# A fourth chunk of x turned by VectorE blocks and carried inside SBUF by GpSimd's queue

## The chip, the cores and the metric

One Trainium2 chip, one core of it. The metric is device time in microseconds (us) for one launch; lower is better. Engines are named as the profile names them: PE (TensorE matmul), PEld (its weight load), DVE (VectorE), ACT (ScalarE), POOL (GpSimd), SP (SyncE, which here only issues DMAs; SPq is its queue).

## The reference

One layer of a hybrid encoder on x of 512 tokens by 2048 channels, all float32. What matters here is the head of it:

```python
def rms_norm(x, w):
    xf = x.astype(jnp.float32)
    y = xf * lax.rsqrt(jnp.mean(xf * xf, axis=-1, keepdims=True) + EPS)
    return (y * w.astype(jnp.float32)).astype(x.dtype)

def hybrid_layer(x, norm_w, w_in, ...):
    h = rms_norm(x, norm_w)                       # (1, 512, 2048)
    proj = jnp.einsum('bsd,de->bse', h, w_in)     # w_in is (2048, 4608)
    q, k, v, g_attn, xr, g_lru = jnp.split(proj, SPLITS, axis=-1)
    attn_out = attention_group(q, k, v, q_norm_w, k_norm_w)
    lru_out = lru_group(xr, conv_w, conv_b, ...)
    mixed = jnp.concatenate([rms_norm(attn_out, attn_norm_w) * jax.nn.silu(g_attn),
                             rms_norm(lru_out, lru_norm_w) * jax.nn.silu(g_lru)], axis=-1)
    return x + jnp.einsum('bse,ed->bsd', mixed, w_out)
```

## The kernel before

Every float32 product is made of three matmuls: both operands are split into a rounded high part and a low rest, and high by high, high by low and low by high are added up in PSUM (`mm3`, L152 to L155). The matmul contracts over the partitions, so x, which lies in memory with tokens on rows, has to be turned: 2048 channels become 16 tiles of 128 channels by 512 tokens. Two tiles are one **chunk**, so x has chunks 0 to 7, and so have the weights of a projection. Chunk c of x is loaded by `xload` (L234 to L241, 512 KB), chunk c of the weights by `wraw` (L206, 512 KB).

The first projection (`proj_feat` with C_XR, the loop at L1212) uses the chunks in order: chunks 0 and 1 by the lines L383 to L396, each later one as 24 matmuls of 512 columns (four column blocks e = 0 to 3 of six matmuls each, L401 to L406). It needs x as its loads arrive, so it begins at the start of the program; all later projections use the same turned x again. Its four sums stand in four PSUM banks named pj, which the second projection takes over when `evac_bc` (L464 to L473, the multiplication at L471) has read them.

There are two ways to turn a chunk:

- `xturn` (L249): PE transposes eight blocks of 128 by 128 into two PSUM banks (L253); ACT writes the high part of x times norm_w (L258), DVE the low part (L261). Chunks 0 to 4 go this way (`TURNED = 5`).
- by blocks (`xchunk`, L317 to L340), chunks 5 to 7: DVE turns blocks of 32 by 32 inside SBUF (`blocks`, L281, four instructions a chunk). What is left is to move blocks between groups of 32 partitions. `put_aside` (L289, tile xd) writes the chunk to HBM, and `bring_back` (L296, four DMAs) reads it back in the right order. Then ACT scales it by norm_w (L338, two instructions), ACT rounds the high parts and DVE subtracts the low ones (L339).

ACT and DVE split the weights: `wsplit` has a cast (L218, tile wh) and a subtraction (L219, tile wl) for each 128 rows. `behind` and `issue_after` only fix the order on an engine. The squares for the norm (`xsquare`) are made on DVE for chunks below TURNED (L272) and on ACT for the others (L268); `xstats` makes rstd from them (L373, L346, L347) and `rows` spreads it over the partitions with two matmuls (L367) into the tile rbc, which the multiplication at L471 needs.

The order around all this is written by hand. SP, PE, ACT and DVE stand in program order there, and the table `moves` (L1195) says what is emitted behind each step (c, e) of the first projection: "x5" advances the generator of chunk 5 to its next `yield`, "w5" issues the load of weight chunk 5, "s5" emits its split. SP issues its DMAs in that order; a DMA that has to wait holds up all behind it. In particular the four DMAs of `bring_back` wait until `put_aside` has landed.

Of the kernel before, what the change touches and what calls it, by code (L numbers as in the profile page):

```python
# [36 lines left out]
AHEAD = 600  # L37
# [12 lines left out]


B = 32
TURNED = 5
NQ = P // B


# [7 lines left out]
def hybrid_kernel(  # L64
# [20 lines left out]
    nc = tc.nc  # L85
# [57 lines left out]
    def mm():  # L143
        return ps.tile([P, SEQ], F32, tag="mm", name=nm("mm"))
# [4 lines left out]
    def f(ap):  # L149
        return ap.bitcast(F32)  # L150
# [7 lines left out]
    ident = const([P, P], "ident")  # L158
# [23 lines left out]
    nw = const([P, KT], "nw")  # L182
# [26 lines left out]
    turn_of, split_done = [0], {}  # L209
# [19 lines left out]

    xh, xl = [None] * KT, [None] * KT  # L230
    ssq = const([P, NT, KT // 2], "ssq")
    highs, x_parts, squared = {}, [], []

    def xload(c, nk=1):  # L234

# [7 lines left out]
    def behind(those):  # L243
        stack = ExitStack()
        for ins in those:
            stack.enter_context(tc.issue_after(ins))
        return stack

    def xturn(xc, kk, then=None):  # L249
        pt = mm()  # L250
        for t in range(NT):
            ks = slice(kk % 2 * P, (kk % 2 + 1) * P)
            nc.tensor.transpose(pt[:, t * P : (t + 1) * P], xc[:, t, ks], ident)  # L253
        if then:
            then()
        xh[kk], xl[kk] = x2(), x2()
        with behind(split_done[-1] if kk > 3 else ()):
            highs[kk // 2] = nc.scalar.activation(  # L258
                xh[kk], pt, AF.Identity, scale=nw[:, kk : kk + 1]
            ).ins  # L260
        nc.vector.scalar_tensor_tensor(  # L261
            xl[kk], pt, nw[:, kk : kk + 1], f(xh[kk]), op0=ALU.mult, op1=ALU.subtract
        )

    def xsquare(xc, c):
        for t in range(NT):
            if c >= TURNED:
                nc.scalar.activation(  # L268
                    xc[:, t, :], xc[:, t, :], AF.Square, accum_out=ssq[:, t, c : c + 1]
                )  # L270
                continue
            square = nc.vector.scalar_tensor_tensor(  # L272
                xc[:, t, :], xc[:, t, :], 1.0, xc[:, t, :], op0=ALU.mult, op1=ALU.mult,
                accum_out=ssq[:, t, c : c + 1],
            )
            if c == 1:
                squared.append(square.ins)

    def blocks(u, t, src):

        nc.vector.transpose(  # L281
            u[:, :, :, t, :].rearrange("p b k r -> p k b r"),
            src.rearrange("p (k b c) -> p k b c", k=2, c=B),
        )

    def put_aside(u, tag, bufs):

        aside_ = dram.tile([P, NQ, 2 * SEQ // NQ], F32, name=nm(tag), tag=tag, bufs=bufs)
        nc.sync.dma_start(aside_, u.rearrange("p b k t r -> p b (k t r)"))  # L289
        return aside_  # L290

    def bring_back(to, aside_):

        src = aside_.rearrange("(i c) b x -> b c i x", c=B)
        for b in range(NQ):
            nc.sync.dma_start(  # L296
                to[b * B : (b + 1) * B].rearrange("p i k t r -> p i (k t r)"), src[b]
            )

    def in_order(v):  # L300
        return v.rearrange("p (t i r) -> p i t r", t=NT, i=NQ)

    def xchunk(c):
# [16 lines left out]
        with tc.high_priority(AHEAD), tc.issue_after(squared[-1] if c == TURNED else split_done[3][1]):  # L320
            for t in range(NT):
                blocks(u, t, xc[:, t, :])
# [9 lines left out]
        with tc.high_priority(AHEAD), behind(split_done[-1]):  # L332
            for k in range(2):
                kk = 2 * c + k
                xh[kk], xl[kk] = x2(), x2()
                hi, lo = (in_order(v) for v in (xh[kk], xl[kk]))
                v = back[:, :, k]
                nc.scalar.activation(v, v, AF.Identity, scale=nw[:, kk : kk + 1])  # L338
                x_parts[:] = nc.scalar.copy(hi, v).ins, nc.vector.tensor_sub(lo, v, f(hi)).ins  # L339
        yield  # L340
# [11 lines left out]
    def rows(dst, col, dg):  # L352

        shape = [P, NT, P]
        part = [const([P, NT], nm("part")) for _ in range(2)]
        parts = [dg() for _ in part]
        nc.vector.tensor_copy(part[0].bitcast(F32R), col)
        nc.vector.tensor_sub(part[1], col, part[0])
        for c, d in zip(part, parts):
            nc.vector.tensor_mul(  # L360
                d, ident[:, None, :].broadcast_to(shape), c[:, :, None].broadcast_to(shape)
            )
        yield
        pb = mm()
        for k, d in enumerate(parts):
            d = d.rearrange("p t q -> p (t q)")
            nc.tensor.matmul(pb, ones_r, d, start=k == 0, stop=k == 1)  # L367
        nc.vector.tensor_copy(dst, pb)
        yield

    def xstats():
        s = const([P, NT], "xsum")
        nc.vector.reduce_sum(s, ssq, axis=AX.X)  # L373
        rsqrt_mean(rstd, s, DM, NT)
        yield from rows(rbc, rstd, lambda: k2(F32R, (P, NT, P)))


# [784 lines left out]
    s2 = ExitStack()  # L1162
# [28 lines left out]
    def split_x(c):  # L1191
# [1 line left out]
            given[c] = [wsplit(raws[c], k) for k in range(2)]  # L1193

    moves = {  # L1195
# [6 lines left out]
    }  # L1202

    def move(step):
# [7 lines left out]
    for step in proj_feat(C_XR, a1, first, given):  # L1212
        if step is None:
            with tc.high_priority():
                first.append(wsplit(raw, 1, nc.vector.tensor_copy))
                xturn(xc, 1)
            xsquare(xc, 0)
            move(None)
            given[1] = wload(w_in, 2 * P, C_XR)
            continue  # L1220
        c, e = step
        move(step)
        if (c, e) == (1, 2):
# [6 lines left out]
        if (c, e) in ((4, 3), (KT // 2 - 1, 0)):  # L1230
            with tc.high_priority(AHEAD), tc.issue_after(split_done[-1][1]):
                next(stats)

    s1.close()
# [214 lines left out]
```

## Time and profile before

| what | value |
|---|---|
| median of 3 runs | 627.18 us (627.06 to 629.06) |
| the profiled execution | 626.85 us |
| its span in the profile | 625.1 us, so 1.75 us lie outside of the span |
| granted TensorE clock | 0.999 |
| PE busy | 619.9 us |
| DVE, ACT, POOL busy | 494.5, 352.5, 101.7 us |

How to read the rows: a timeline row gives the start, the duration, the engine, the line of the kernel, the operation, the tile written and the tiles read, shapes, and how many instructions in a row were merged (x8); a bracket tells how long the engine had been idle before and what ended that. Buffer numbers are left out of tile names, so that every chunk of x is "b" when loaded, "xu" when in blocks, "xd" in HBM and "x" when split. Matmuls are pipelined: the distance between two starts says what one costs, not its duration. In rows of waits stand the total, the number of times and the longest.

### The profile page before, as it was taken

Reading aid. Unit: us, or ns where it says so; the run is one execution under the profiler, and the core shown is the slowest. Engines: PE = TensorE matmul, PEld = TensorE weight load, DVE = VectorE, ACT = ScalarE, POOL = GpSimd, SP = SyncE. Lnnn points to the kernel's source line nnn. Section 1 sums busy time; section 2 is a strip of 40 time slices with the busy share of each in tenths; the row PEclk is TensorE's granted clock in tenths of the full one; section 3 lists DMA queues with packets and bytes.
Section 4 is the critical chain, followed back from the end, with each engine's and each line's share of the span. In section 5 each row is a group of like instructions: output and inputs, shape, how many; then the busy total and the mean of one; then the engine's idle time right before and its main releaser. Section 6 shows DMA issues by size and latency. Waiting matters only on the chain.

```text
span 625.1 us, 8277 instructions
## 1 busy us (share of the span) xinstructions
PE 619.9 (99%) x2756; PEld 512.5 (82%) x2756; DVE 494.5 (79%) x796; ACT 352.5 (56%) x617; POOL 101.7 (16%) x134
## 2 busy tenths in 40 slices
PE   9999999999999999999999999999999999999997
PEld 7888888888888888888888888888888888888886
DVE  5967979986699875987887888549978866886886
ACT  3764899379935823555475447428445633443441
POOL 0000211112003622622122222100310101010010
PEclk9999999999999999999999999999999999999999
DMA  8987775859774599489668646923995676896262
GB/s 289 303 227 224 182 198 171 179 134 198 233 232 139 169 245 242 104 204 271 187 179 254 201 143 192 265 76 107 270 243 183 209 253 228 297 339 226 70 202 101
DMA packets 73595, 127.61 MB, mean 204 GB/s; under 512 B 6617, under 2 KB 29265, under 8 KB 73553
## 3 DMA queue, kind: packets, MB, share of 16 engines
q1 hardware_dynamic: 65664, 109.65, 56.8%
q0 software_dynamic: 7712, 17.31, 14.3%
q8 instruction: 21, 0.34, 0.2%
q14 instruction: 22, 0.17, 0.1%
q10 hardware_dynamic: 176, 0.14, 0.1%
HBM read 110.29 MB, written 37.75 MB: 237 GB/s over the span
## 4 chain that ended last, share of the span: by engine, by line
PE 99%; ACT 0%; DVE 0%; issue 0%; POOL 0%; POOLq 0%
PE pj L153 20%; PE pj L155 20%; PE pj L154 20%; PE mm L1029 14%; PE pj L1029 11%; PE mm L155 3%; PE mm L153 3%; PE mm L154 3%; PE pj L388 2%; PE mm L253 1%; PE mm L1156 0%; PE mm L829 0%; ACT x L258 0%; PE mm L367 0%; DVE cb L1058 0%
## 5 line engine op out<-in xcount | busy, mean ns | idle before, releaser
L153 PE MATMUL pj<-x,wh 128*128 128x512 f32 x368 | 143.5, 390 | 0.0
L155 PE MATMUL pj<-x,wl 128*128 128x512 f32 x368 | 143.2, 389 | 0.0
L154 PE MATMUL pj<-x,wh 128*128 128x512 f32 x368 | 143.2, 389 | 0.0
L218 ACT CAST wh<-wr 128x512 fp32r<-128x512 f32 x142 | 84.5, 617 | 79.3 <-PE pj L154 31.7
L219 DVE TENSOR_TENSOR wl<-wr,wh 128x512 fp32r<-128x512 f32 x144 | 99.5, 720 | 19.6 <-ACT wh L218 18.5
L881 ACT CAST wh<-wr 128x1024 fp32r<-128x1024 f32 (+1 forms) x72 | 60.7, 861 | 75.0 <-PE mm L1029 37.5
L882 DVE TENSOR_TENSOR wl<-wr,wh 128x1024 fp32r<-128x1024 f32 (+1 forms) x72 | 68.7, 984 | 30.3 <-ACT wh L881 30.0
L155 PEld LDWEIGHTS pj<-x,wl 128*128 128x128 f32 x368 | 69.1, 188 | 14.5
L154 PEld LDWEIGHTS pj<-x,wh 128*128 128x128 f32 x368 | 69.1, 188 | 14.3
L153 PEld LDWEIGHTS pj<-x,wh 128*128 128x128 f32 x368 | 69.1, 188 | 14.2
L153 PE MATMUL pj<-wh,x 128*128 128x512 f32 x192 | 74.7, 389 | 0.0
L155 PE MATMUL pj<-wh,x 128*128 128x512 f32 x192 | 74.7, 389 | 0.0
L154 PE MATMUL pj<-wl,x 128*128 128x512 f32 x192 | 74.7, 389 | 0.0
L905 POOL DMA_DIRECT2D t<-in_w_out_dram x40 | 33.6, 906 | 157.7 <-DMA t<-in_w_out_dram 99.9
L1029 PE MATMUL mm<-wh,ml 128*128 128x512 f32 x126 | 49.0, 389 | 0.0
L1029 PE MATMUL mm<-wh,mh 128*128 128x512 f32 x126 | 49.0, 389 | 0.0
L1029 PE MATMUL mm<-wl,mh 128*128 128x512 f32 x126 | 49.0, 389 | 0.0
L154 PEld LDWEIGHTS pj<-wl,x 128*128 128x128 f32 x192 | 36.0, 188 | 7.6
L155 PEld LDWEIGHTS pj<-wh,x 128*128 128x128 f32 x192 | 36.0, 188 | 7.5
L153 PEld LDWEIGHTS pj<-wh,x 128*128 128x128 f32 x192 | 36.0, 188 | 7.4
L706 POOL TENSOR_SCALAR p<-p,sm 128x512 f32<-128x512 f32 x32 | 24.3, 762 | 89.3 <-DVE sm L705 89.3
L1029 PE MATMUL pj<-wl,mh 128*128 128x512 f32 (+1 forms) x100 | 38.5, 385 | 0.0
(201 smaller groups left out, 1050.8 us busy)
## 6 DMA issues: line engine op xcount, KB each, us to landing
wr<-in_w_in_dram SPq DMA_DIRECT2D x71, 512.0 KB, 5.0
wr<-in_w_out_dram SPq DMA_DIRECT2D x24, 512.0 KB, 5.2
t<-in_w_out_dram POOLq DMA_DIRECT2D x40, 256.0 KB, 7.3
wr<-t SPq DMA_DIRECT2D x40, 256.0 KB, 5.6
pd<-u SPq DMA_DIRECT2D x16, 512.0 KB, 3.0
pt<-pd SPq DMA_DIRECT2D x64, 128.0 KB, 3.9
t<-in_w_out_dram SPq DMA_DIRECT2D x24, 256.0 KB, 5.3
t<-t SPq DMA_DIRECT2D x16, 256.0 KB, 5.4
```

Of the source, the lines that this page charges most:

```text
L153: nc.tensor.matmul(acc, lh, rh, start=start, stop=False)
L154: nc.tensor.matmul(acc, lh, rl, start=False, stop=False)
L155: nc.tensor.matmul(acc, ll, rh, start=False, stop=stop)
L218: copy(hi, raw[:, k, :]).ins,
L219: nc.vector.tensor_sub(lo, raw[:, k, :], f(hi)).ins,
L253: nc.tensor.transpose(pt[:, t * P : (t + 1) * P], xc[:, t, ks], ident)
L388: nc.tensor.matmul(acc[e], w[:, e * P : (e + 1) * P], x_[2 * c + k], start=c == k == j == 0, stop=False,)
L706: last_pool[0] = nc.gpsimd.tensor_scalar(p, p, sm, 0.0, op0=ALU.mult, op1=ALU.add).ins
L881: nc.scalar.copy(hi[:, to], b)
L882: nc.vector.tensor_sub(lo[:, to], b, f(hi[:, to]))
L905: nc.gpsimd.dma_start(dst, src, accum_op=ALU.add)
L1029: nc.tensor.matmul(dst[s][:, es], lh[:, ts_], rh[:, es], start=i == ends_[0] and j == 0, stop=i == ends_[1] and j == 2,)
```

## The change

Chunk 4 is turned by DVE's blocks as chunks 5 to 7 are (`TURNED = 4`), but `carry` moves its blocks from SBUF to SBUF: twelve DMAs of 32 KB on GpSimd's queue for the blocks that change their group of partitions, and four ACT copies for those that stay. Its squares are now made on ACT. The scaling by norm_w of chunks 4 to 7 is done by GpSimd (`tensor_scalar_mul`) instead of ACT. The first tile of x is transposed into two PSUM banks, and scaled and split in two halves of 256 tokens. The table `moves`, and with it the order of the loads, is written anew; the three chunks that go through HBM now go one after the other. In the first projection's last chunk the two matmuls of `rows` move from behind e = 0 to behind e = 1, where the transpose that makes `vec` stands; that one now stands ahead of them.

```diff
-TURNED = 5
+TURNED = 4
...
-    def xturn(xc, kk, then=None):
+    def xturn(xc, kk, then=None, n=1):
+        xh[kk], xl[kk] = x2(), x2()
+        ks = slice(kk % 2 * P, (kk % 2 + 1) * P)
+        parts_ = []
+        for h in range(n):
+            pt, w = mm(), SEQ // n
+            for t in range(NT // n):
+                nc.tensor.transpose(pt[:, t * P : (t + 1) * P], xc[:, h * NT // n + t, ks], ident)
+            cols = slice(h * w, (h + 1) * w)
+            with behind(split_done[-1] if kk > 3 else ()):
+                highs[kk // 2] = nc.scalar.activation(
+                    xh[kk][:, cols], pt[:, :w], AF.Identity, scale=nw[:, kk : kk + 1]
+                ).ins
+            parts_.append((pt[:, :w], cols))
...
+    def carry(to, u):
+
+        def at_(v, b):
+            return v[b * B : (b + 1) * B]
+
+        for d in range(1, NQ):
+            for b in range(NQ):
+                i = (b + d) % NQ
+                nc.gpsimd.dma_start(at_(to, b)[:, i], at_(u, i)[:, b])
+        with behind(split_done[2]):
+            for b in range(NQ):
+                nc.scalar.copy(at_(to, b)[:, b], at_(u, b)[:, b])
...
         with tc.high_priority(AHEAD):
-            there = put_aside(u, "xd", KT // 2 - TURNED)
-        with tc.issue_after(highs[TURNED - 1]):
-            xsquare(xc, c)
-        yield
-        with tc.high_priority(AHEAD):
-            bring_back(back, there)
+            if c == TURNED:
+                carry(back, u)
+            else:
+                there = put_aside(u, "xd", KT // 2 - TURNED - 1)
+                yield
+                bring_back(back, there)
...
-                nc.scalar.activation(v, v, AF.Identity, scale=nw[:, kk : kk + 1])
+                scaled[:] = (nc.gpsimd.tensor_scalar_mul(v, v, nw[:, kk : kk + 1]).ins,)
                 x_parts[:] = nc.scalar.copy(hi, v).ins, nc.vector.tensor_sub(lo, v, f(hi)).ins
...
-        xturn(xc, 0, split_first)
+        xturn(xc, 0, split_first, 2)
...
-        None: "x1", (0, 2): "x1",
+        None: "x1", (0, 2): "x1 x2 x4",
...
```

Where instructions stand now. First SP, from the load of weight chunk 4 (wr_383 before, wr_344 in the change) on. xd is a chunk on its way to HBM, "xu from xd" its way back; before, the chunks are 5 (xd_399), 6 (xd_431) and 7 (xd_437), and wr_405, wr_411 and wr_483 are the weights of chunks 5, 6 and 7:

```order
L206 DMA wr_383<-in_w_in_dram 128x2x512
L289 DMA xd_399<-xu_331 128x1024
L206 DMA wr_405<-in_w_in_dram 128x2x512
L296 DMA xu_332<-xd_399 32x4x256 x4
L206 DMA wr_411<-in_w_in_dram 128x2x512
L289 DMA xd_431<-xu_419 128x1024
L289 DMA xd_437<-xu_425 128x1024
L296 DMA xu_420<-xd_431 32x4x256 x4
L206 DMA wr_483<-in_w_in_dram 128x2x512
L296 DMA xu_426<-xd_437 32x4x256 x4
```

The same place in the change, where chunks 5, 6 and 7 are xd_378, xd_428 and xd_456, their weights wr_430, wr_454 and wr_492, b_61 is chunk 7 of x and wr_749 the first weights of the second projection:

```order
L206 DMA wr_344<-in_w_in_dram 128x2x512
L293 DMA xd_378<-xu_372 128x1024
L240 DMA b_61_386<-in_x_dram 128x4x256
L300 DMA xu_373<-xd_378 32x4x256 x4
L293 DMA xd_428<-xu_418 128x1024
L206 DMA wr_430<-in_w_in_dram 128x2x512
L300 DMA xu_419<-xd_428 32x4x256 x4
L206 DMA wr_454<-in_w_in_dram 128x2x512
L293 DMA xd_456<-xu_438 128x1024
L206 DMA wr_749<-in_w_in_dram 128x2x512
L300 DMA xu_439<-xd_456 32x4x256 x4
L206 DMA wr_492<-in_w_in_dram 128x2x512
```

Before, chunks 6 and 7 were put aside together, so that SP waited for two landings; in the change each chunk is put aside only when the one ahead of it has been asked back, and SP waits for three.

POOL, from its first DMA on, in the change (before, none of these rows stood ahead of the one that writes rstd):

```order
L312 DMA xu_256<-xu_255 32x256 x12
L367 TENSOR_SCALAR xu_256<-xu_256,nw 128x4x128 x2
L367 TENSOR_SCALAR xu_373<-xu_373,nw 128x4x128 x2
L367 TENSOR_SCALAR xu_419<-xu_419,nw 128x4x128 x2
L367 TENSOR_SCALAR xu_439<-xu_439,nw 128x4x128 x2
L379 TENSOR_SCALAR rstd<-xsum 128x4
```

Chunk 4's twelve DMAs and the eight scalings of chunks 4 to 7 came onto this queue.

Last DVE, where it reads the first projection's four banks (pj) into the tiles ev. Before:

```order
L471 TENSOR_TENSOR ev_694<-pj_159,rbc 128x512
L471 TENSOR_TENSOR ev_696<-pj_160,rbc 128x512
L471 TENSOR_TENSOR ev_698<-pj_161,rbc 128x512
L509 SCALAR_TENSOR_TENSOR k_122_706<-ev_694,vec,k_122_706 128x510
L471 TENSOR_TENSOR ev_700<-pj_162,rbc 128x512
```

In the change, from behind the copy of rbc on:

```order
L505 TENSOR_TENSOR ev_711<-pj_162,rbc 128x512
L534 TENSOR_TENSOR k_122_720<-k_113_699,k_121_719 128x512
L505 TENSOR_TENSOR ev_713<-pj_163,rbc 128x512
L543 SCALAR_TENSOR_TENSOR k_123_723<-ev_711,vec,k_123_723 128x510
L219 TENSOR_TENSOR wl_786<-wr_783,wh_785 128x512
L219 TENSOR_TENSOR wl_790<-wr_783,wh_789 128x512
L543 SCALAR_TENSOR_TENSOR k_123_723<-ev_711,vec,k_123_723 128x511
L505 TENSOR_TENSOR ev_715<-pj_164,rbc 128x512
L543 SCALAR_TENSOR_TENSOR k_123_723<-ev_711,vec,k_123_723 128x511
L505 TENSOR_TENSOR ev_717<-pj_165,rbc 128x512
```

The third read (ev_715) stood two instructions behind the first one; now it stands seven behind.

More of the change, by code (lines that the diff above doesn't have):

```diff
@@ L247, in behind @@
         return stack
-    def xturn(xc, kk, then=None):
[L250 to L253, printed above, removed]
+    def xturn(xc, kk, then=None, n=1):
[12 more added lines that the diff above has]
+            parts_.append((pt[:, :w], cols))
         if then:
             then()
[L256 to L259, printed above, removed]
+        for pt, cols in parts_:
+            lows[kk // 2] = nc.vector.scalar_tensor_tensor(
+                xl[kk][:, cols], pt, nw[:, kk : kk + 1], f(xh[kk][:, cols]),
+                op0=ALU.mult, op1=ALU.subtract,
             ).ins
-        nc.vector.scalar_tensor_tensor(
-            xl[kk], pt, nw[:, kk : kk + 1], f(xh[kk]), op0=ALU.mult, op1=ALU.subtract
-        )
     def xsquare(xc, c):
@@ L319, in xchunk @@
         )
[L320 removed]
+        raw_x[c] = xc
+        with tc.high_priority(AHEAD), behind(lows_of(c)):
             for t in range(NT):
[L322 removed]
+                blocked[c] = blocks(u, t, xc[:, t, :])
         yield
         with tc.high_priority(AHEAD):
[L325 to L327 removed]
+            if c == TURNED:
[4 more added lines that the diff above has]
+                bring_back(back, there)
+        if c == TURNED:
+            with tc.issue_after(highs[c - 1]):
+                xsquare(xc, c)
         yield
[L329 to L332 removed]
+        with tc.high_priority(AHEAD), behind(
+            (*split_done[-1], blocked[TURNED + 1]) if c == TURNED else split_done[-1]
+        ):
             for k in range(2):
@@ L337, in xchunk @@
                 v = back[:, :, k]
-                nc.scalar.activation(v, v, AF.Identity, scale=nw[:, kk : kk + 1])
+                scaled[:] = (nc.gpsimd.tensor_scalar_mul(v, v, nw[:, kk : kk + 1]).ins,)
                 x_parts[:] = nc.scalar.copy(hi, v).ins, nc.vector.tensor_sub(lo, v, f(hi)).ins
+        yield
+        for n in {5: (5, 6), 6: (7,)}.get(c, ()):
+            with behind(split_done[c][:1]):
+                xsquare(raw_x[n], n)
         yield
@@ L374, in xstats @@
         rsqrt_mean(rstd, s, DM, NT)
+        yield
         yield from rows(rbc, rstd, lambda: k2(F32R, (P, NT, P)))
@@ L1229, in hybrid_kernel @@
             columns(vec, vec_st)
-        if (c, e) in ((4, 3), (KT // 2 - 1, 0)):
-            with tc.high_priority(AHEAD), tc.issue_after(split_done[-1][1]):
+        if (c, e) in ((5, 3), (6, 3), (KT // 2 - 1, 1)):
+            with tc.high_priority(AHEAD), behind((split_done[-1][1], *scaled)):
                 next(stats)
```

14 lines of the change are left out of this document (8 added, 6 removed), and 10 rows, old and new, of the table moves.

## The prediction

> **What bounds the kernel now.** I read the page's busy times and chain first, then PE's waits, then the timeline of the first 56 us, where all changed instructions stand.
>
> ```profile
> PE 619.9 (99%) x2756; PEld 512.5 (82%) x2756; DVE 494.5 (79%) x796; ACT 352.5 (56%) x617; POOL 101.7 (16%) x134
> PE 99%; ACT 0%; DVE 0%; issue 0%; POOL 0%; POOLq 0%
> ...
> PE mm L1156 <- POOL ones L161: 1.1, 1, 1.1
> ```
>
> The second row is the chain that ended last, by engine; the third is the whole table of PE's waits. PE is busy from its first instruction to the end, and nothing but the first constant makes it wait. So a microsecond of PE work taken out is a microsecond won, and anything else matters only where it makes PE wait. After the 56 us discussed here the engines' orders are those of before but for a pair of DVE instructions, so I look for losses only there.
>
> **What is won.** The chunk that leaves PE:
>
> ```profile
> 22.39 0.39 PE L155 MATMUL pj<-x,wl 128*128 128x512 f32 x1
> 22.62 1.03 PE L253 MATMUL mm<-ident,b 128*128 128x128 f32 x8
> 23.41 0.48 PE L153 MATMUL pj<-x,wh 128*128 128x512 f32 x1
> ...
> 47.76 0.39 PE L155 MATMUL pj<-x,wl 128*128 128x512 f32 x1
> 47.99 0.39 PE L153 MATMUL pj<-x,wh 128*128 128x512 f32 x1
> ```
>
> Between two matmuls without transposes lie 0.23 us (47.76 to 47.99), with eight transposes 1.02 (22.39 to 23.41). Chunk 4's eight go: **−0.79 us**.
>
> The first tile's halves:
>
> ```profile
> 3.81 1.11 PE L253 MATMUL mm<-ident,b 128*128 128x128 f32 x4
> ...
> 4.71 0.85 PE L1156 MATMUL mm<-ones 128*128 128x256 bf16 x3
> 4.96 0.69 ACT L258 ACTIVATE x<-mm,nw 128x512 fp32r<-128x512 f32 x1 [2.25 <-PE mm L253]
> ...
> 5.70 1.23 PE L388 MATMUL pj<-x,wh 128*128 128x512 f32 x4
> ```
>
> ACT now waits for four transposes, then scales for 0.69 us, and PE starts 0.05 later. With halves it may begin two transposes earlier, and only half of the scaling stands behind the last one: at best half of 0.69, 0.35 us. An instruction on half the columns costs more than half, and the three warm-up matmuls hold PE until 5.56, so at worst 0.14 (5.70 to 5.56) or, if something else is late, nothing. I take **−0.2** (0 to −0.35). Both together: PE would be 0.99 ahead, and reach chunk 7 of the first projection at 47.99 − 0.99 = 47.0.
>
> **What may be late: the way through HBM.** In SP's timeline, L289 writes a chunk to HBM, L296 asks it back, L206 loads weights:
>
> ```profile
> 17.50 0.34 SPq L289 DMA_DIRECT2D xd<-xu  x1
> ...
> 24.77 1.76 SPq L296 DMA_DIRECT2D xu<-xd  x4
> 26.63 0.39 SPq L206 DMA_DIRECT2D wr<-in_w_in_dram  x1
> 27.12 0.88 SPq L289 DMA_DIRECT2D xd<-xu  x2
> 33.21 1.74 SPq L296 DMA_DIRECT2D xu<-xd  x4
> ...
> 35.55 1.83 SPq L296 DMA_DIRECT2D xu<-xd  x4
> ...
> SPq L296 <- DMA xd<-xu: 9.5, 2, 5.1
> pd<-u SPq DMA_DIRECT2D x16, 512.0 KB, 3.0
> ```
>
> The last two rows are SP's wait for the landing (twice), and the median landing of a later transfer of the same kind and size. Writing to asking back took 7.3 us behind a full queue (17.50 to 24.77) and 6.1 behind four reads and a load (27.12 to 33.21); alone it can be 3.0. What follows the asking:
>
> ```profile
> 29.28 1.34 ACT L338 ACTIVATE xu<-xu,nw 128x512 f32<-128x512 f32 x2 [0.20 <-DMA xu<-xd]
> ...
> 38.06 1.34 ACT L338 ACTIVATE xu<-xu,nw 128x512 f32<-128x512 f32 x2 [3.76 <-DMA xu<-xd]
> 39.30 1.13 ACT L339 CAST x<-xu 128x512 fp32r<-128x512 f32 x2
> 40.33 1.14 ACT L218 CAST wh<-wr 128x512 fp32r<-128x512 f32 x2
> 41.74 1.34 ACT L338 ACTIVATE xu<-xu,nw 128x512 f32<-128x512 f32 x2 [0.26 <-DMA vec_st<-in_lru_norm_w_dram]
> ```
>
> From asking to use are 4.5 us (24.77 to 29.28), 4.85 (33.21 to 38.06) and 6.2 (35.55 to 41.74, behind earlier reads and a load). From there to the weights' first cast, without which PE cannot begin the chunk, are 2.85 (38.06 to 40.33, and half of 1.14).
>
> Now the chain in the new order. Chunk 5's blocks stand on DVE behind the same splits as these seven of chunks 6 and 7 did, but for one block that stands earlier:
>
> ```profile
> 22.41 2.39 DVE L281 STREAM_TRANSPOSE xu<-b 128x256 f32<-128x256 f32 x7
> ```
>
> Ahead of ACT's casts there stand three of the new small copies, an estimated 0.3 us each; so the last three blocks (0.34 each) run from about 23.2 to 24.3. From there: write 3.0 (the queue is drained by then), 27.3; four reads issued, 1.85, and chunk 6 is put aside at 29.15. It lies behind those reads, so I take 4.2, between 3.0 and 6.1: asked back at 33.35. Reads and one load issued, 2.25: chunk 7 is put aside at 35.6. It lies behind four reads and a load, as the 6.1 did, but the load is later in the queue: 5.4 (3.0 to 7.3). Asked back at 41.0, landed after 4.7 (4.5 to 6.2) at 45.7, ready for PE 2.85 later at 48.55. PE is there at 47.0: **+1.55 us of waiting**. With all low ends the chunk is ready at 44.75 and nothing waits; with all high ends at about 54, 7 us late. Chunk 5, by the same steps ready at 34.9, and 6, ready at 40.9, are due at 36.1 and 41.55: hidden, with about a microsecond to spare.
>
> GpSimd scales instead of ACT:
>
> ```profile
> L905 POOL DMA_DIRECT2D t<-in_w_out_dram x40 | 33.6, 906 | 157.7 <-DMA t<-in_w_out_dram 99.9 <-issue 39.1 <-DMA t<-t 18.5
> L706 POOL TENSOR_SCALAR p<-p,sm 128x512 f32<-128x512 f32 x32 | 24.3, 762 | 89.3 <-DVE sm L705 89.3
> ...
> L1053 POOL DMA_DIRECT2D out_dram<-xt x6 | 3.4, 572 | 74.5 <-DVE xt L1104 57.4 <-DVE xt L1058 17.0
> ...
> t<-in_w_out_dram POOLq DMA_DIRECT2D x40, 256.0 KB, 7.3
> ...
> out_dram<-xt POOLq DMA_DIRECT2D x6, 256.0 KB, 4.0
> ```
>
> Two scalings of 0.76 us take the place of ACT's 1.34, and ACT's first cast runs beside the second: nothing, so the 2.85 stays. ACT's freed time has no price either, nor have the extra squares there: it was idle for 3.76 us before the second use above.
>
> **Chunk 4's carrying.** Its blocks follow the squares of chunk 1:
>
> ```profile
> 14.40 0.42 DVE L272 SCALAR_TENSOR_TENSOR b<-b 128x256 f32<-128x256 f32 x1
> ...
> 16.05 1.42 DVE L281 STREAM_TRANSPOSE xu<-b 128x256 f32<-128x256 f32 x4 [1.23 <-DMA b<-in_x_dram]
> ```
>
> DVE is free at 14.8 (the four blocks before waited 1.23 us for an x that is now one place later in the queue), so they are done at 16.2. A DMA issue on POOL costs 0.572 us for a plain write out of SBUF and 0.906 for an adding one in HBM; landing takes 4.0 and 7.3. None of before goes from SBUF to SBUF with 32 KB. I take the plain row, which it is nearest to: 16.2 + 12 × 0.572 + 4.0 = 27.1, and with 2.85 ready at 29.95; due at 47.99 − 0.99 − 3 × 24 × 0.227 = 30.7. Hidden by 0.7. By the other ends 16.2 + 10.9 + 7.3 + 2.85 = 37.2, 6.5 us late.
> [...] No row of before shows POOL's queue beside a full one.
>
> **The reading of the banks.** The second projection needs the four pj banks one after the other, 6 × 0.227 = 1.36 us apart.
>
> ```profile
> 49.35 0.62 PE L367 MATMUL mm<-k,ones_r 128*128 128x512 f32 x2
> 50.01 0.69 DVE L368 COPY rbc<-mm 128x512 f32<-128x512 f32 x1 [3.89 <-PE mm L367]
> ...
> 52.59 1.87 DVE L471 TENSOR_TENSOR ev<-pj,rbc 128x512 f32<-128x512 f32 x3
> 54.39 0.74 DVE L509 SCALAR_TENSOR_TENSOR k<-ev,vec,k 128x510 f32<-128x510 f32 x1
> 55.05 0.68 DVE L471 TENSOR_TENSOR ev<-pj,rbc 128x512 f32<-128x512 f32 x1
> ```
>
> The copy of rbc begins 0.66 after the pair of matmuls. Call X the start of the change's transpose ahead of that pair, which costs about 0.1: the copy starts at X + 0.76. DVE's steps are 0.6 to 0.66 apart by these rows, so the third read, eight steps on, ends at about X + 6.4. PE has the pair (0.46) and 12 matmuls, and is at the second projection's third block at X + 0.56 + 24 × 0.227 = X + 6.0: **+0.4 us** (0 to 1). Before, the fourth read ended at 55.7, and PE came to that bank at about 58. Whether X itself is late doesn't matter to this.
>
> **Sum** against the profiled execution of 626.85 us (the span of 625.1 and 1.75 around it): −0.79 − 0.2 + 1.55 + 0.4 = +0.96, 627.8. The median of the runs shown lies 0.33 above that execution, so I forecast **628.2**. About 0.3% (1.9 us) is what a measurement can tell from no change.
>
> **Rivals.**
> 1. *The trips fit.* If each write lands as the 3.0 row says, chunk 7 is ready in time; what is left is −0.99 and +0.4: 626.3, or 626.6 on the median. For it speaks that a write from SBUF is quick alone; against, that both trips in the trace took over 6.
> 2. *GpSimd's queue is the late one.* Twelve issues follow one another on one engine, and the chunk is due 14.5 us after its blocks. It turns the sum to slower by more than 0.3% once the blocks land after about 30.2, that is 14.0 us behind the last DVE block, or 0.83 us an issue with a landing of 4.0. With 0.906 and 7.3 it is 6.5 late: 626.85 − 0.99 + 0.4 + 6.5 = 632.8, on the median 633.1. For it: 40 of POOL's DMAs cost 0.906. Against: those add in HBM.
> 3. *The trips are as long as those measured* (6.1 and 7.3 for the second and third): ready at 24.3 + 3 + 1.85 + 6.1 + 2.25 + 7.3 + 4.7 + 2.85 = 52.35, 5.35 late; 631.6, on the median 631.9.
> [...]
>
> **How the numbers follow.** Forecast 0.50; rival 1 0.22; rival 2 0.12; rival 3 0.13; rival 4 0.03. The range 626.0 to 630.6 goes from rival 1 with the halves worth 0.35 and a cheap bank reading to the parts of rivals 2 and 3 that are less than half as bad as written; their worse parts and rival 4 stay out. Slower by over 0.3%: rival 4, and most of 2 and 3, 0.25; faster 0.01, since no more than 1.14 us is to be won; the same 0.74.
>
> **What would show it.** No transposes inside the first projection's chunk 2 (22.62 above); its first matmul near 5.5; SP asking chunks 5, 6, 7 back near 27, 33 and 41; PE waiting for ACT ahead of chunk 7 and for DVE at the second projection's third bank. [...] The forecast is wrong if chunk 5 or 6 is already late, or if PE waits anywhere after 60 us.

## The result, and the profile after

The changed kernel takes **634.49 us** (median of 5 runs, 633.9 to 635.12), the kernel before 627.18 beside it: a ratio of 1.0109 (95% interval 1.0094 to 1.0124), 1.1% slower. The forecast was 628.2, with a range up to 630.6. In the profiled execution the span grew from 625.1 to 632.0 us, 6.9 us.

The page of the changed kernel, busy times and chain:

```profile
PE 622.2 (98%) x2748; PEld 511.7 (81%) x2748; DVE 495.6 (78%) x793; ACT 352.1 (56%) x624; POOL 121.4 (19%) x154
...
PE 90%; DMA 2%; DVE 1%; POOL 1%; issue 1%; ACT 0%; SPq 0%; POOLq 0%; ACTq 0%; DVEq 0%
```

PE has eight matmuls less and is busy 2.3 us longer, and the chain has left PE for a tenth of the span. The table of PE's waits had one entry before; now (total, times, longest):

```profile
PE pj L153 <- ACT wh L218: 3.4, 2, 2.5
PE mm L1190 <- POOL ones L161: 1.1, 1, 1.1
PE pj L422 <- ACT x L259: 0.4, 1, 0.4
PE pj L1063 <- DVE ev L505: 0.4, 1, 0.4
PE pj L153 <- DVE ev L505: 0.4, 1, 0.4
PE mm L256 <- DMA b<-in_x_dram: 0.2, 1, 0.2
```

The two waits for ACT's casts of weights stand ahead of chunk 5 (1.0 us) and of chunk 7. The waits for ev are the second projection's third bank and a bank at 477 us; the rest lies at the start. PE's timeline around the second, and the clock there (busy times by engine, then PEclk, the DMA share and GB/s):

```profile
48.80 0.39 PE L155 MATMUL pj<-x,wl 128*128 128x512 f32 x1
51.71 0.50 PE L153 MATMUL pj<-x,wh 128*128 128x512 f32 x1 [2.52 <-ACT wh L218]
52.05 0.53 PE L154 MATMUL pj<-x,wh 128*128 128x512 f32 x1
...
53.10 0.63 PE L153 MATMUL pj<-x,wh 128*128 128x512 f32 x1
53.53 0.63 PE L154 MATMUL pj<-x,wh 128*128 128x512 f32 x1
...
55.62 0.39 PE L153 MATMUL pj<-x,wh 128*128 128x512 f32 x1
55.86 0.39 PE L154 MATMUL pj<-x,wh 128*128 128x512 f32 x1
```

```profile
53.00:54.00 1.00, 1.00 (x4) 0.71 (x4) 1.00 (x5) 0.21 (x1) 0.00 (x0) 0.50 1.10 323
...
56.00:58.00 2.00, 2.00 (x11) 1.61 (x10) 1.35 (x5) 0.10 (x1) 0.00 (x0) 1.00 0.97 291
```

Between 48.80 and 51.71 PE loses 2.7 us, and then the matmuls come 0.43 us apart instead of 0.23: the granted clock is 0.50 until about 55.5. So the wait is followed by a second loss: the next nine distances take 3.91 us in all (51.71 to 55.62), where 9 × 0.227 = 2.04 is usual. How much of these 1.87 us is the clock's, the first experiment shows.

What made chunk 7 late, on SP (put aside, a load of the second projection, asked back), GpSimd (scaling) and ACT (casts):

```profile
36.12 0.41 SPq L293 DMA_DIRECT2D xd<-xu  x1
38.93 0.38 SPq L206 DMA_DIRECT2D wr<-in_w_in_dram  x1
42.83 1.74 SPq L300 DMA_DIRECT2D xu<-xd  x4
```

```profile
16.52 4.11 POOL L312 DMA_DIRECT2D xu<-xu  x8 [14.82 <-DVE xu L285]
22.68 1.96 POOL L312 DMA_DIRECT2D xu<-xu  x4 [2.05 <-DMA xu<-xu]
26.24 3.12 POOL L367 TENSOR_SCALAR xu<-xu,nw 128x512 f32<-128x512 f32 x2 [1.59 <-DMA xu<-xu]
...
47.38 3.10 POOL L367 TENSOR_SCALAR xu<-xu,nw 128x512 f32<-128x512 f32 x2 [5.50 <-DMA xu<-xd]
```

```profile
48.98 0.62 ACT L368 CAST x<-xu 128x512 fp32r<-128x512 f32 x1 [3.79 <-DMA vec_st<-in_lru_bx_dram]
50.52 0.62 ACT L368 CAST x<-xu 128x512 fp32r<-128x512 f32 x1 [0.92 <-POOL xu L367]
51.04 2.17 ACT L218 CAST wh<-wr 128x512 fp32r<-128x512 f32 x4
```

Two scalings take 3.10 us, and ACT's second cast waits for the second one. The 6.9 us of the span, against the terms of the forecast:

| term | forecast | measured |
|---|---|---|
| PE begins chunk 7 (47.99 before) | 48.55 | 51.71 |
| of that: put aside at | 35.6 | 36.12 |
| put aside to asked back | 5.4 | 6.71 (36.12 to 42.83) |
| asked back to first use | 4.7 | 4.55 (42.83 to 47.38) |
| first use to PE | 2.85 | 4.33 (47.38 to 51.71) |
| nine slow distances after the wait | none | +1.87 |
| second projection's third bank | +0.4 | +0.53 |
| wait for a bank at 477 us | none | +0.53 |

Chunk 7 begins 3.72 later than before (51.71 against 47.99): 3.72 + 1.87 + 0.53 + 0.53 = 6.65. The other 0.25 is spread over small gaps. Against the forecast, chunk 7 is 3.16 late: 0.52 by the putting aside, 1.31 by the trip, 1.48 from first use to PE, and −0.15 by the way back.

### The profile page after: what moved, and what is told of

Same layout as the page of the kernel before. It is cut to its first block, busy times and chain, and to the rows that moved or that the text cites. A ratio compares the mean times of both kernels' runs of the same rounds, so it can differ in the third digit from the quotient of the medians.

```text
span 632.0 us, 8307 instructions
## 1 busy us (share of the span) xinstructions
PE 622.2 (98%) x2748; PEld 511.7 (81%) x2748; DVE 495.6 (78%) x793; ACT 352.1 (56%) x624; POOL 121.4 (19%) x154
## 4 chain that ended last, share of the span: by engine, by line
PE 90%; DMA 2%; DVE 1%; POOL 1%; issue 1%; ACT 0%; SPq 0%; POOLq 0%; ACTq 0%; DVEq 0%
PE pj L153 19%; PE pj L155 19%; PE pj L154 19%; PE mm L1063 13%; PE pj L1063 11%; PE mm L155 3%; PE mm L154 3%; PE mm L153 3%; DMA xd<-xu 1%; POOL xu L367 1%; DMA xu<-xd 0%; DVE wl L219 0%; DVE b L278 0%; DVE ev L505 0%; SPq L300 0%
## 5 line engine op out<-in xcount | busy, mean ns | idle before, releaser
L1063 PE MATMUL pj<-wh,mh 128*128 128x512 f32 (+1 forms) x100 | 38.6, 386 | 0.4 <-DVE ev L505 0.4
```

Source lines behind the costliest of these rows:

```text
L1063: nc.tensor.matmul(dst[s][:, es], lh[:, ts_], rh[:, es], start=i == ends_[0] and j == 0, stop=i == ends_[1] and j == 2,)
```

## The experiments

Each quoted block says what was expected of a run. Times are medians, with the lowest and the highest in brackets.

### Scaling back on ACT, and a PE that isn't left idle

```diff
-                scaled[:] = (nc.gpsimd.tensor_scalar_mul(v, v, nw[:, kk : kk + 1]).ins,)
+                nc.scalar.activation(v, v, AF.Identity, scale=nw[:, kk : kk + 1])
```

> The changed kernel with the scaling of chunks 4 to 7 back on ACT, all else kept. Theory A (GpSimd's scaling is dear, 1.56 us each where I had 0.76, and stands on the path of chunks 5 and 7): chunk 7's first cast of weights comes 2.85 us after the chunk's last landing instead of 4.3, so PE begins chunk 7 about 1.5 us earlier (50.2 instead of 51.7); the wait ahead of chunk 5 (1.0 us) goes, but that time only moves into the wait ahead of chunk 7, which stays at 2.5 us or more, with the low clock behind it. About 633.0 us. Rival B (both waits cost their own): 631.5 us. Rival C (the scaling is beside other work, as I forecast): 634.5 us.

And, between chunks 6 and 7:

```diff
+        if (c, e) == (6, 3):
+            warm = mm()
+            busy(20)
```

> The changed kernel with 20 matmuls of 128x256 bf16 on constants, whose result nobody reads, on PE between chunks 6 and 7 of the first projection, where it waits 2.5 us in the changed kernel. Theory A (the low granted clock of 0.5 from 52 to 55.6 us comes from PE's idle time just before, and doubles the time of the ten matmuls that follow, 0.43 us apart instead of 0.23): these run 0.23 apart, the clock stays at 1.0, and the kernel is 2.0 us faster, 632.5 us. Rival B (the ten matmuls are slow because transfers, casts and splits of weights run beside them): nothing changes, 634.5 us, or slower if the 20 matmuls take longer than the wait (0.11 to 0.23 us each, 2.2 to 4.6 us).

Measured: 633.2 us (631.56 to 635.83) with ACT's scaling, 633.08 (632.04 to 633.54) with the 20 matmuls. PE in the latter:

```profile
50.90 2.36 PE L1190 MATMUL mm<-ones 128*128 128x256 bf16 x20
53.01 0.48 PE L153 MATMUL pj<-x,wh 128*128 128x512 f32 x1
53.32 0.40 PE L154 MATMUL pj<-x,wh 128*128 128x512 f32 x1
53.55 0.39 PE L155 MATMUL pj<-x,wl 128*128 128x512 f32 x1
```

Chunk 7's matmuls come 0.23 apart, with the same casts and transfers beside them, so these did not make them slow; rival B is out. That the idle time did is likely, but this run alone doesn't show it: in this execution chunks 5 and 6 were later, PE came to chunk 7 at 50.90 instead of 49.03, and the wait would have been about 1.3 us only (ACT's first cast of the weights began at 51.57, and PE starts 0.67 behind it in the changed kernel). The 20 matmuls held PE until 53.01, some 0.8 longer, and so only 1.4 us of the 2.0 appear in the time.

With ACT's scaling the wait ahead of chunk 5 went (0.16 left), but chunk 7 began at 51.53, not at 50.2: asked back at 42.88, it was used only from 48.60 on, 5.7 us later instead of 4.55. A 0.6 us wait ahead of chunk 6 was new, since ACT's scaling there stood behind eight squares, and the second projection's bank made PE wait 1.35 us instead of 0.53. The clock, after a wait as long as before (48.62 to 51.53):

```profile
53.00:54.00 1.00, 1.00 (x6) 0.80 (x5) 1.00 (x4) 0.04 (x1) 0.00 (x0) 1.00 0.00 0
```

It stayed at 1.00, where the changed kernel had 0.50. The nine distances behind the wait took 2.65 us here (51.53 to 54.18), 0.61 over the usual at full clock; by this comparison some 1.3 of the 1.87 us are the clock's. The low clock follows such a wait in one execution (0.50) and not in another (1.00), so the 1.3 us won on the median can't be put down to the scaling alone. Theory A had the right sum by a partly wrong way.

### Which form of the scaling

```diff
-                scaled[:] = (nc.gpsimd.tensor_scalar_mul(v, v, nw[:, kk : kk + 1]).ins,)
+                scaled[:] = (nc.gpsimd.tensor_scalar(
+                    v, v, nw[:, kk : kk + 1], 0.0, op0=ALU.mult, op1=ALU.add
+                ).ins,)
...
-        last_pool[0] = nc.gpsimd.tensor_scalar(p, p, sm, 0.0, op0=ALU.mult, op1=ALU.add).ins
+        last_pool[0] = nc.gpsimd.tensor_scalar_mul(p, p, sm).ins
```

> The changed kernel with GpSimd's two kinds of scaling exchanged: chunks 4 to 7 by a multiply and an add of zero (the form of the scaling of p in the attention, 0.7 us), p by a multiply alone (the form used for the chunks, 1.56 us). Theory A (the form of the instruction makes the difference): the chunks' scaling takes 0.7 to 0.8 us, that of p 1.5, and the attention is later for it. Rival B (the way through memory makes it, four pieces of 128 elements instead of 512 in a row): the chunks' scaling stays at 1.55 us, p's at 0.7. Rival C (transfers or DVE beside it make it): neither stays as it was.

GpSimd's groups (busy time, mean ns of one), in the changed kernel and with the forms exchanged:

```profile
L740 POOL TENSOR_SCALAR p<-p,sm 128x512 f32<-128x512 f32 x32 | 24.2, 760 | 89.6 <-DVE sm L739 89.6
L367 POOL TENSOR_SCALAR xu<-xu,nw 128x512 f32<-128x512 f32 x8 | 13.2, 1658 | 12.6 <-DMA xu<-xd 11.1 <-DMA xu<-xu 1.6
```

```profile
L742 POOL TENSOR_SCALAR p<-p,sm 128x512 f32<-128x512 f32 x32 | 52.8, 1654 | 83.7 <-DVE sm L741 81.4 <-PE pj L154 2.3
...
L367 POOL TENSOR_SCALAR xu<-xu,nw 128x512 f32<-128x512 f32 x8 | 6.3, 801 | 17.3 <-DMA xu<-xd 15.7 <-DMA xu<-xu 1.6
```

Theory A is shown, on both tiles: the multiply alone takes twice as long as the multiply with an added zero (1658 against 801 ns for the chunks, 1654 against 760 for p, on average). The attention pays for it (651.5 us, one run). My row for the forecast, 762 ns, was of the other form.

With only the chunks' form put right, and the multiplications that read the banks given precedence:

```diff
-        with tc.high_priority():
+        with tc.high_priority(2 * AHEAD):
             for n, a in enumerate(acc):
```

> The changed kernel with one word of its edit put right: chunks 4 to 7 scaled on GpSimd by a multiply and an add of zero (0.8 us) instead of a multiply alone (1.56 us), and the bank reads given precedence on DVE. The way through HBM stays as the change has it. Theory A (the scaling is 1.5 us of chunk 5's and of chunk 7's path, the third trip the rest): the wait ahead of chunk 5 shrinks from 1.0 to 0.5 us or less, PE begins chunk 7 at 50.2 to 50.7 instead of 51.7 after a wait that is still over 2 us; with the bank's 0.5 won, 632.5 us where that wait brings the low clock and 631 where it doesn't. Rival B (the transfers alone set when chunk 7 comes): no more than the bank's 0.5 is won, 634 us.

Measured: 633.34 us (632.91 to 633.48). The wait ahead of chunk 5 is gone and the second projection's bank waits no more. But chunk 7, asked back at 43.35, was used from 49.40 on, and PE waited 3.2 us for it; the mean granted clock of this execution was 0.997, as in the changed kernel. The time lies between theory A's 632.5 and rival B's 634; PE begins chunk 7 at 51.98, as late as before, and in this rival B is right: the transfers set when chunk 7 comes.

### Fewer trips in a row

Chunks 6 and 7 put aside together, as in the kernel before, with x's chunk 7 loaded earlier and later loads of weights held in place; then the same with ACT's scaling:

```diff
-        (2, 0): "x6 w4 x4", (2, 1): "x5 x5", (2, 2): "x7", (2, 3): "s3 x4",
-        (3, 0): "x6 x5 x6 w5", (3, 1): "x7 x6", (3, 2): "w6 x7", (3, 3): "s4 x5",
-        (4, 0): "x7 w7", (4, 3): "s5 x5 x6",
+        (2, 0): "x6 x7 w4 x4", (2, 1): "x5 x5", (2, 3): "s3 x4",
+        (3, 0): "x6 x7 x5 x6 w5 x7", (3, 1): "x6", (3, 2): "w6 x7", (3, 3): "s4 x5",
+        (4, 0): "w7", (4, 3): "s5 x5 x6",
```

> The changed kernel with chunks 6 and 7 put aside one right after the other (x's chunk 7 loaded earlier, its blocks behind those of chunk 6; two loads of weights held behind the load for chunk 6 and the last read of chunk 7), so that the way through HBM is made two times after one another instead of three. GpSimd still scales. Theory A (the third trip in a row, asked back at 42.8 us, is what makes chunk 7 late): SP asks chunk 7 back at about 37.5, PE does not wait ahead of it, the clock stays at 1.0, and only the wait ahead of chunk 5 (1.0 to 1.5 us, by GpSimd's scaling), the second projection's bank and 0.5 late in the kernel are left: 629 us (628 to 630.5). Rival B (the bytes ahead in the queue set it, not the number of trips): chunk 7 lands as late as before, 634 us.

> As the kernel with chunks 6 and 7 put aside together, and the scaling back on ACT. Theory A (the two named costs, trip and scaling, are all that makes PE wait in the first projection): no wait above 0.3 us ahead of chunks 4 to 7, 0.8 us of transposes won, and the second projection's bank (0.5 us) left: 627.0 us, within 0.3% of the kernel before. Rival B (carrying chunk 4 or the other order of casts has a price of its own): over 629 us.

Measured: 651.7 and 646.52 us. The experiment hit something else. PE and DVE of the second, far behind the place of the edit:

```profile
126.79 0.69 DVE L507 TENSOR_TENSOR ev<-pj,rbc 128x512 f32<-128x512 f32 x1
```

```profile
127.53 0.80 PE L153 MATMUL pj<-wh,x 128*128 128x512 f32 x1 [13.17 <-DVE ev L507]
```

DVE's order there is set by a scheduler, and with other loads early on it put two multiplications that read banks behind a whole recurrence; PE waited 13 us. For that reason the kernels below have the precedence for those reads. The first 60 us still tell something: SP asked chunk 7 back at 40.20 only, since two loads of weights ahead of it took 4.1 us (36.05 to 40.14), and chunk 4 was late for the first time, by 1.5 us ahead of it and inside it, with x's chunk 7 loaded beside its carrying.

Then the smaller step: only chunk 7's putting aside moves ahead of chunk 6's asking back; with ACT's scaling; and with the squares spread:

```diff
-(3, 0): "x6 x5 x6 w5", (3, 1): "x7 x6", (3, 2): "w6 x7", (3, 3): "s4 x5"
+(3, 0): "x6 x5 x6 w5", (3, 1): "x7 x7 x6", (3, 2): "w6", (3, 3): "s4 x4 x5"
...
-        for n in {5: (5, 6), 6: (7,)}.get(c, ()):
+        for n in {4: (5,), 5: (6,), 6: (7,)}.get(c, ()):
```

> The changed kernel with chunk 7 put aside ahead of asking chunk 6 back (instead of behind that and the load of chunk 6's weights), the later loads of weights held in the order of the changed kernel, and the reads of the banks given precedence on DVE, so that the order of casts and blocks late in the kernel stays what it was and no bank is read late. GpSimd still scales. Theory A (the third trip in a row, behind the bytes of two other transfers, makes chunk 7 late by 2.7 us, and that wait brings the low clock): SP asks chunk 7 back at about 39.3 instead of 42.8, PE waits under 0.5 us ahead of it, the clock stays at 1.0, the wait ahead of chunk 5 (1 to 1.5 us, GpSimd's scaling) stays: 634.5 - 2.7 - 2.0 - 0.5 = 629.3 us. Rival B (bytes, not the trip: the reads of chunk 7 then stand behind two loads of weights): chunk 7 is as late as before and only the bank's 0.5 is won, 634 us.

> As the kernel with chunk 7 put aside early and the bank reads given precedence, and the scaling of chunks 4 to 7 back on ACT. Theory A (GpSimd's scaling costs 0.8 us more an instruction than I had, on the path of each chunk): the wait ahead of chunk 5 (1 to 1.5 us) goes; ahead of chunk 6 0.6 us may be left, where ACT's scaling now stands behind eight squares: 628.0 to 628.8 us. Rival B (the scaling is not what chunk 5 waits for, but its trip): the same time as with GpSimd's scaling.

> As the last, and the squares of chunks 5 and 6 on ACT one chunk earlier each (four behind each chunk's casts instead of eight behind chunk 5's). Theory A (with trip, scaling, squares and banks mended nothing in the first 60 us makes PE wait): the eight transposes of chunk 4 are won, 0.8 us, and nothing else differs from the kernel before: 626.4 us against its 627.2, a ratio of 0.9985 or so. Rival B (the carrying through GpSimd's queue has a price that the other waits hid, chunk 4 ready late): PE waits ahead of chunk 4, 627.5 us or more.

Measured: 634.81, 631.04 and 630.62 us (the last 628.9 to 632.65, ratio to before 1.0048, 1.003 to 1.0066). So theory A fell for the first and for the last. For ACT's scaling it holds by direction (3.8 us between the first two, though 628.0 to 628.8 was expected). In the profile of the first, chunk 4 was 2.5 us late as well, so that not all of it is the scaling. The kernel that was to be free of waits, ACT, SP, and the window of 40 to 45 us:

```profile
36.20 1.14 ACT L218 CAST wh<-wr 128x512 fp32r<-128x512 f32 x2 [0.87 <-DMA wr<-in_w_in_dram]
...
46.94 1.34 ACT L369 ACTIVATE xu<-xu,nw 128x512 f32<-128x512 f32 x2 [1.88 <-DMA vec_st<-in_lru_bx_dram]
```

```profile
36.08 2.48 SPq L206 DMA_DIRECT2D wr<-in_w_in_dram  x2
38.61 1.88 SPq L302 DMA_DIRECT2D xu<-xd  x4
```

```profile
40.00:45.00 5.00, 4.77 (x20) 3.32 (x19) 2.50 (x4) 4.96 (x14) 0.00 (x0) 1.00 1.06 257
```

Chunk 7 is asked back 4.2 us earlier than in the changed kernel and used 0.4 us earlier: 8.3 us lie between, and chunk 5's weights land late as well. Two loads of weights, 1 MB, stood ahead of the reads in SP's queue; that the early asking was worth little because of them is my estimate. The trace has the reads' 1 KB packets from 41.1 to 45.6, with the DMA engines at 1.06. One of the two loads is chunk 6's; the other is the second projection's first, which PE needs only behind chunk 7. No run moved that one behind the reads. Chunk 7 in all these kernels:

| kernel | asked back | first use | PE begins chunk 7 |
|---|---|---|---|
| before | 35.55 | 41.74 | 47.99 |
| changed | 42.83 | 47.38 | 51.71 |
| ACT's scaling | 42.88 | 48.60 | 51.53 |
| quick form on GpSimd | 43.35 | 49.40 | 51.98 |
| put aside early | 41.89 | 50.51 | 54.84 (late already) |
| the same, ACT's scaling | 40.56 | 47.30 | 51.72 (late already) |
| the same, squares spread | 38.61 | 46.94 | 49.88 |

### Where the transfers' time went

Windows of 20 to 25 us, of the kernel before and of the changed one (the last two columns are the DMA engines' busy share and GB/s):

```profile
20.00:25.00 5.00, 5.00 (x28) 4.22 (x27) 5.00 (x12) 3.02 (x8) 0.00 (x0) 1.00 0.94 354
```

```profile
20.00:25.00 5.00, 5.00 (x25) 4.13 (x24) 4.31 (x10) 4.78 (x14) 2.59 (x6) 1.00 0.43 113
```

Before, chunk 5 was put aside at 17.50, and the engines stayed full (0.94); now they are half idle (0.43) until it is put aside, at 24.55, and what follows stands closer together (a share of 0.87 from 25 to 40 us, 0.83 before). So, on the last kernel, chunk 5's blocks on DVE ahead of chunk 3's low parts:

```diff
-        (1, 3): "x3",
+        (1, 3): "x5 x3",
...
-        for pt, cols in parts_:
-            lows[kk // 2] = nc.vector.scalar_tensor_tensor(
+        with behind((blocked[5],) if kk > 5 else ()):
+            for pt, cols in parts_:
+                lows[kk // 2] = nc.vector.scalar_tensor_tensor(
```

> As the kernel with trip, scaling (ACT), squares and banks mended, and chunk 5's four blocks made on DVE ahead of the low parts of chunk 3, at about 20.3 to 21.7 us instead of 24 to 25. Theory A (what is left of the loss is that the changed kernel leaves the DMA engines idle from 19 to 24 us and then pushes 5.5 MB through them until chunk 7 is due): chunk 5 is put aside 3.5 us earlier, near 21.8, all three chunks come in time, PE's waits ahead of chunks 5 to 7 are under 0.3 us together and the clock stays at 1.0: 626.5 to 627.2 us. Rival B (the DMA engines stay full anyway, each chunk behind the weights of the chunk before): chunk 7 as late as in the kernel it is made from, 630 us.

> As the kernel with chunk 5's blocks made early, with GpSimd's scaling by a multiply and an add in place of ACT's. Theory A (in its quick form the scaling on GpSimd costs nothing, as the forecast had it): the same time as with ACT's scaling, within 0.5 us. Rival B (each hand-over between GpSimd and ACT costs, so that the chunks come 0.5 to 1 us later): 1 us slower.

Measured: 632.31 us (631.07 to 632.59) and 631.93 (631.2 to 632.02). Chunk 5 was put aside at 23.07 instead of 25.33 (21.8 was expected), and what it won chunk 4 lost. The first is 1.7 us slower than the kernel it is made from, and most of that may be the clock's: its profiled run, with a mean granted clock of 1.0, took 631.07, the three others, with 0.996 to 0.997, took 632.21 to 632.59. ACT, and PE's waits, of the first:

```profile
28.88 1.34 ACT L370 ACTIVATE xu<-xu,nw 128x512 f32<-128x512 f32 x2 [3.84 <-DMA xu<-xu]
```

```profile
PE pj L155 <- DVE wl L219: 2.0, 2, 1.8
...
PE pj L153 <- ACT wh L218: 1.0, 1, 1.0
```

Chunk 4's carried blocks, used from 26.77 on in the kernel it is made from, are there at 28.88, though GpSimd had issued them 0.6 us earlier, and PE waits ahead of chunk 4 and inside it (the latter because DVE, late with chunk 4, makes chunk 7's blocks ahead of its low parts of weights). GpSimd's quick form and ACT's scaling give the same time (0.4 us apart): in the quick form GpSimd's scaling has no price, as the forecast had it.

Last, which transfers it is: without chunk 7's way through HBM on the one kernel, without chunk 4's carrying on the other, their blocks used in the order in which DVE leaves them:

```diff
             if c == TURNED:
                 carry(back, u)
+            elif c == 7:
+                back = u
+                yield
```

> As the kernel with trip, scaling (ACT), squares and banks mended, but chunk 7 isn't put aside and brought back at all: its blocks are used as DVE leaves them (that part of the exchange is left out). Theory A (the 3 us that are left stand in transfers: 1 MB of them goes here): no wait ahead of chunk 7, and less ahead of 5 and 6, since SP's queue is shorter: 626.5 to 628 us. Rival B (what is left are orders on ACT and DVE): ahead of chunk 7 PE waits as before, 0.9 us or more, and the time stays near 630.

```diff
-                carry(back, u)
+                back = u
```

> As the kernel with chunk 5's blocks made early, but chunk 4 isn't carried from SBUF to SBUF: its blocks are used as DVE leaves them (that exchange, twelve transfers on GpSimd's queue and four copies on ACT, is left out). Theory A (the carried blocks and chunk 5's way through HBM take the same DMA engines, and chunk 4 was late because chunk 5 was put aside earlier): the waits ahead of chunk 4 and within it (1.2 and 2.0 us) go, and nothing new comes: 628 us or less against 632.3. Rival B (DVE's and ACT's order makes chunk 4 late, not its landing): they stay.

Measured: 627.96 us (626.74 to 629.27; ratio to before 1.0004, 0.9992 to 1.0015) and 628.51 (627.16 to 629.3; 1.0011, 0.9999 to 1.0023). PE's waits, of the first and of the second:

```profile
PE mm L1195 <- POOL ones L161: 1.1, 1, 1.1
PE pj L1068 <- DVE ev L510: 0.4, 1, 0.4
PE pj L427 <- ACT x L261: 0.3, 1, 0.3
PE mm L258 <- DMA b<-in_x_dram: 0.2, 1, 0.2
```

```profile
PE mm L1193 <- POOL ones L161: 1.1, 1, 1.1
PE pj L1066 <- DVE ev L508: 0.4, 1, 0.4
```

These are all of PE's waits: those ahead of chunks 4 to 7 are gone in both. In the first, the small waits of chunks 5 and 6 (0.24 and 0.16 us) went too, though those chunks weren't touched; but chunk 5 was put aside 0.76 us earlier in this execution (24.57 against 25.33), which the edit doesn't bring. In the second nearly all the waiting had been at chunk 4 itself, and for the 2.0 us inside it DVE's order has a part that this run doesn't separate. So it is shown that the loss comes with the exchanges: with one of the four left out, by either way, PE waits for none. It is not shown whether the bytes do it or their order on SP's queue, nor that four chunks can't be carried in another order.

### The halves alone

```diff
-        xturn(xc, 0, split_first)
+        xturn(xc, 0, split_first, 2)
```

> The kernel before with the first tile of x scaled in two halves and nothing else. Theory A (PE begins 0.2 to 0.3 us earlier, but the second tile's transposes wait for the same load as before, so it is given back): 627.2 us, no change, the first matmul at 5.45 and the second tile's transposes at 6.75. Rival B (what I forecast): 0.2 us faster.

Measured: 628.05 us against 627.17, a ratio of 1.001 (1.0001 to 1.0019): nothing won, rather 0.6 us lost by the ratio.

```profile
5.35 1.21 PE L394 MATMUL pj<-x,wh 128*128 128x512 f32 x4 [0.38 <-ACT x L259]
6.96 0.66 PE L256 MATMUL mm<-ident,b 128*128 128x128 f32 x4 [0.40 <-DMA b<-in_x_dram]
```

PE starts 0.35 us earlier, four matmuls later it stands before the second tile, whose x lands at its own time, and it goes on at 6.96, 0.2 later than before (6.76). The rest of the loss is elsewhere: this kernel also has the wait of 0.53 us late in the kernel that is told of below.

## Why the prediction was wrong

- **Eight transposes less, −0.79:** right. Chunk 3 began 0.82 us earlier (25.41 against 26.23), though chunk 2 had begun 0.07 later.
- **Halves, −0.2:** wrong, shown by the halves alone. I priced PE's start and not what it waits for next, the load of the second tile.
- **"Nothing, so the 2.85 stays" for GpSimd's scaling:** this step failed. The 0.76 us came from a row of another form of the instruction; the form that the change uses takes 1.57. From first use to PE it became 4.33 us instead of 2.85 for chunk 7, and 4.86 for chunk 5 (32.68 to 37.54), which came 1.0 late where the forecast had called it hidden, "with about a microsecond to spare". Mended, in two ways, the time changes by little over 1 us (633.2 and 633.34), since the transfers are late too.
- **The third trip, 5.4 + 4.7:** this step failed as well. 6.71 + 4.55 came out, which the ends 3.0 to 7.3 and 4.5 to 6.2 held, so the trip was mis-sized by 1.31 us. The putting aside was 0.52 late, 0.25 of it from chunk 5: no row stood behind the 0.3 us for ACT's small copies, and they took 0.40. Behind that stands a picture that was too simple: I gave each trip a length from a row and never added up what the DMA engines had to move between 20 and 47 us, nor saw that the new order leaves them half idle first. Asked back 4.2 us earlier, behind 1 MB of weights, chunk 7 was used only 0.4 earlier; with a whole exchange left out, PE waited for no chunk.
- **The carrying, hidden:** right for the kernel as changed (GpSimd's first scaling at 26.24, forecast 27.1), in part by luck. The twelve issues took 8.1 us (16.52 to 24.64) instead of 6.9, with a wait of 2.05 for an earlier landing among them, and the last blocks were there 1.6 us later instead of 4.0. The 4.0 is from another kind of transfer, and for blocks carried beside loads on SP's queue no run shows it: I had taken the two ways as independent, which was my assumption. The runs showed 1.6 us in the changed kernel and 4.2 in the kernel with early blocks (24.69 to 28.88), where chunk 5 was put aside at 23.07 and PE waited 1.05 us ahead of chunk 4. So the carried blocks can be the late ones, as rival 2 had it; what in the transfers makes them late is not shown.
- **The bank, +0.4:** right, 0.53.
- **What no term had:** the slow matmuls after the wait, 1.87 us, of which some 1.3 are the granted clock's; and a wait of 0.53 us at 477, where the forecast looked for losses in the first 56 us only. Its own signs of being wrong came: chunk 5 was late, and PE waited after 60 us. At 477 DVE reads the banks after two low parts of weights:

```profile
476.19 1.23 DVE L916 TENSOR_TENSOR wl<-wr,wh 128x1024 fp32r<-128x1024 f32 x1 [0.48 <-ACT wh L915]
477.33 2.48 DVE L505 TENSOR_TENSOR ev<-pj,rbc 128x512 f32<-128x512 f32 x4
```

This wait stands in every trace of this study but the one of the kernel before, also in that with the halves alone. What brings it stays open, and with a single trace of the kernel before it isn't known whether that kernel is free of it in every execution.

Of the rivals the second (633.1) came near in time, but by luck: GpSimd's issues took 0.51 us each, not 0.906, and PE didn't wait ahead of chunk 4. For the fourth, which got a chance of 0.03, the runs show nothing: the first eight issues stood 0.51 us apart while DVE was busy for 4.13 of the 5 us from 15 to 20. By its mechanism the third, trips as long as those measured, was nearest, with 631.9; it lacked the scaling and the clock. No kernel with four carried chunks beat the one before. Even without a wait ahead of any chunk (chunk 7's or chunk 4's exchange left out) the time is no better than before: there the 0.8 us of transposes stand against the wait at 477 and, it seems, the halves.

## What to carry to other kernels

When transfers are moved, add up what the DMA engines must carry in each stretch, look where they fall idle and what stands ahead in the same queue, before any trip is priced by itself. A price from a row holds for that very form of the instruction: here 1566 ns for one form and 696 for the other, on the same shape. And where PE is the bound, a wait may bring a second loss in slow matmuls behind it: here up to 1.9 us behind one of 2.7.

## What the runs showed of the hardware

- GpSimd's TENSOR_SCALAR on 128x512 f32 takes 1566 ns with a multiply alone (median; chunks, changed kernel; p with the forms exchanged 1654 on average), and with a multiply and an add of zero 696 (median; p, changed kernel) and 694 (chunks, quick form).
- The clock after a wait of PE: in the changed kernel 2.7 us of idle time were followed by 0.50 for about 3.5 us (52.05 to 55.6); with ACT's scaling the same 2.7 us were followed by 1.00; in the kernel with chunk 7 put aside early and ACT's scaling, 1.9 us ahead of chunk 5 were followed by 0.50:

```profile
41.00:42.00 1.00, 1.00 (x3) 0.75 (x3) 0.00 (x0) 1.00 (x7) 0.00 (x0) 0.50 0.72 168
```

So in these executions the length of the wait alone does not tell whether the low clock follows it, and what decides it is not shown.
